# A decoder layer on one core: its beginning rearranged, the narrow gate load moved to chunk two, and two modulation sums spread over other units

## The chip, the core and the metric

The kernel runs on one NeuronCore of a Trainium2 chip. Its engines are TensorE (PE: matmuls, and PEld for the weight loads that run beside them), VectorE (DVE), ScalarE (ACT), GpSimd (POOL) and SyncE (SP, which here only issues loads and stores). The metric is the time of one execution on the device in microseconds.

## What is computed

One layer of a hybrid decoder, for one sequence of 256 tokens with 2048 channels, in float32. Cut to what matters:

```python
mod = silu(c) @ w_mod + b_mod                  # (2048) x (2048, 6*2048)
sh_m, sc_m, g_m, sh_f, sc_f, g_f = split(mod, 6)
h = rmsnorm(x, mix_pre_w) * (1 + sc_m) + sh_m
proj = h @ w_in                                # 48 tiles of 128 columns, and 16 more columns: a_lr
y_conv = cb * causal_dwconv3(cc * cx, conv_w)
log_a = log_sigmoid(a_lr @ gate_w2 + gate_b) / 16
y_gla = gla_chunked(q, k, v, log_a)            # then a norm for each head, times silu(r)
x = x + g_m * rmsnorm(concat(y_conv, y_gla) @ w_out, mix_post_w)
h = rmsnorm(x, ffn_pre_w) * (1 + sc_f) + sh_f
g, val = split(causal_dwconv3(h @ w_up, ffn_conv_w), 2)
x = x + g_f * rmsnorm((silu(g) * val) @ w_down, ffn_post_w)
```

All weights are read once from HBM. The modulation vector is needed in six parts: sh_m and sc_m (called the first modulation below) before the first projection, g_m (the second, "g") before the first residual, sh_f and sc_f (the third, "f" and "f2" for its two halves), g_f at the end.

## The kernel before, in words

**Products in three parts.** PE works in a fast format that keeps fewer bits (fp32r). To keep float32 precision each weight is split into a high part (`high`, a cast on ACT, L140) and a low part (`low`, the difference, on DVE, L145), and so are the activations (`act_high`, `act_low`, L380). A product is then high x high, high x low and low x high: L490, L491 and L492 in the input projection, L753 to L755 in the output and down products, L897 and L899 (two halves packed in one) in the up product. A few places use full float32 matmuls, among them L282 (columns of the modulation), L361 (transposes of x) and L436 (the product with the gate's 16 narrow columns, `alr_w`).

**Modulation.** The row of the modulation is summed on DVE: for each of 16 slices j of `w_mod`, one instruction adds c_act[j] times the slice to an accumulator (`mod_steps`, `stt` at L136). Each partition holds a share of the sum; a product with ones (L282) adds the shares and turns the row into columns (`mod_columns`: `products`, then `columns`, L285). For the first modulation this happens in four pieces, one for each chunk of the contraction; the pieces for chunks two to four, and g, f, f2, are spread over units (`spread`), with the list MODS giving the unit numbers at which one ends and the next begins.

**Chunks and units.** The input projection contracts over 2048 channels in four chunks (`CHUNKS`: 2, 4, 5 and 5 tiles of 128 channels). Chunk one runs over all 48 output tiles before chunk two begins. A unit is a group of two to four output tiles in a chunk, with its own weight load. Chunk one has units 0 to 11, chunk two 12 to 23, chunk three 24 to 41, chunk four 42 to 59; units 60 to 75 are the output product, then come the up and down products. A unit of chunk one has 24 matmuls, one of chunk two 48, one of the output product mostly 24 of double width.

**Order.** Every engine runs its instructions in program order, and `drive` writes that order. For unit i it issues: the unit's `early` list (mostly modulation steps), the load and the cast of weight i+2 (`prep`), the low part of weight i+1 (`low`), a `pre` list, the matmuls, a `mid` list, what earlier units have due (`fin`, the evacuation of PSUM), a `late` list. So DVE has the low part of a unit to do while PE works on the unit before, and a modulation step stands ahead of it in the same queue. All large loads are issued by SP in this same order; a load waits until its buffer is free. Loaded weights and modulation slices share six buffers ("raw"); high and low parts have three each ("wh", "wl"); most other tiles are slots of a pool of twenty ("big").

**The beginning.** `steps0` loads and sums the first piece (16 slices, in loads of four and then two slices). x is loaded in two halves of 128 tokens, at steps 0 and 8 (`XLD`), squared and scaled (`norm_squares`, `rstd_of`, L1013 to L1015) after steps 3 and 14 (`NLD`), and its first two tiles are transposed into PSUM. Then come the narrow load of `alr_w` (L1016, 128 partitions x 16 pieces of 64 bytes), the columns, and `modulate_chunk(0)`: ACT scales the transposed tiles (L367), casts them (L376), DVE takes the low part (L380), PE makes the gate's product for this chunk (L436). `drive` begins with the load and split of weight 0 and the load of weight 1.

**Between chunks.** In the unit before the last of a chunk the next chunk's columns are made and the next tiles of x transposed and modulated (`cols`, `mod0`, `LEAD` = 2); behind the last unit stand the low parts of the activations and the gate's products (`second`), and in the middle of the next chunk's first unit their sum (`third`, L446).

Of the kernel before, what the change touches and what calls it, by code (L numbers as in the profile page):

```python
# [36 lines left out]
XLD = (0, 8)  # L37
NLD = (3, 14)
# [3 lines left out]
MODS = (10, 21, 31, 46, 70)  # L42
# [7 lines left out]
NHF = 3  # L50

# [52 lines left out]
def layer_kernel(ctx: ExitStack, tc, x, c, w_mod, b_mod, mix_pre_w, mix_post_w, w_in, conv_w, gate_w2, gate_b,  # L104
# [47 lines left out]
    nc.scalar.activation(c_act, c_sb, AF.Silu)  # L152

# [3 lines left out]
    def mod_steps(s0, n, a, w, nj, first=False):  # L157
# [3 lines left out]
        def step(j):  # L161
            if j == 0:
# [3 lines left out]
                if first:  # L166
                    cur["b"] = slot([1, n, w])
                    nc.gpsimd.dma_start(cur["b"], b_mod_v[:, s0:s0 + n, a:a + w])
                else:
                    nc.gpsimd.memset(acc, 0.0)  # L170
                    nc.gpsimd.dma_start(acc[0:1, :, :], b_mod_v[:, s0:s0 + n, a:a + w])
# [8 lines left out]
            src, cj = cur["r"][:, j % m, :, :], c_act[:, j:j + 1]  # L180
            if first and j == 0:
                nc.vector.tensor_scalar_mul(cur["acc"], src, cj)
            else:
                stt(cur["acc"], src, cj, cur["acc"])
            if first and j == 3:
                nc.vector.tensor_add(cur["acc"][0:1], cur["acc"][0:1], cur["b"])
# [3 lines left out]
    accs0, steps0 = mod_steps(0, 2, 0, CHUNKS[0] * P, 4 if CHUNKS[0] < 3 else 2, True)  # L190

    ident = col(P, "ident")
    nc.scalar.dma_start(ident, ident_in)
# [3 lines left out]
    nc.scalar.copy(ones_r, ones)  # L197
    eps_t = col(1, "eps_t")
    nc.gpsimd.memset(eps_t, EPS)
# [218 lines left out]
    def modulate_chunk(ci, ash, early=None):  # L418
# [3 lines left out]

        def first():
            for kts in pairs(k0, k1):
                ps = early.pop(0) if early else turn_norm(xs, kts)
                hf = hf0[:, kts[0]:kts[-1] + 1, :] if ci == 0 else hf_tile()
# [5 lines left out]
        def second():  # L432
            ps = bank([P, T])
            for kts, hf, parts in kept:
                for i, k in enumerate(kts):
                    nc.tensor.matmul(ps[:16, :], alr_w[:, k, :], hf[:, i, :], start=(k == k0), stop=(k == k1 - 1))  # L436
                if parts:
                    act_low(*parts)
            kept.append(ps)

        def third():
            ps = kept.pop()
            if ci == 0:
                nc.vector.tensor_copy(alr[:16, :], ps[:16, :])
            else:
                nc.vector.tensor_add(alr[:16, :], alr[:16, :], ps[:16, :])  # L446

        return first, second, third

    def in_units(ci):  # L450
# [10 lines left out]
        def unit(tiles, plain):  # L461
# [3 lines left out]
            def prep():  # L465
                r = raw_tile([P, n, m * P])
# [9 lines left out]
            def mm():  # L476
                w = cur["w"]
                for o, nt in enumerate(tiles):
                    if nt // 2 not in banks:
                        banks[nt // 2] = bank([P, 2, T])  # L480
                    ps = banks[nt // 2][:, nt % 2, :]
# [19 lines left out]
        return [unit(g, i in (PLAIN, FULL1, FULL2, FULL)[ci]) for i, g in enumerate(groups)]  # L501
# [501 lines left out]
    for j, f in enumerate(steps0):  # L1003
        f()
        if j in XLD:
            load_x(XLD.index(j))
        if j == 0:
            load_small()
        if j in NLD:
            t = NLD.index(j)  # L1010
            r = rstd_of(norm_squares(t, f"n1{t}"), 4, f"n1{t}")
            e = CHUNKS[0] * P
            nc.vector.tensor_scalar_mul(xs[t][0][:, :e], xs[t][0][:, :e], r)  # L1013
            nc.scalar.activation(xs[t][0][:, e:], xs[t][0][:, e:], AF.Copy, scale=r)
            nc.scalar.activation(xs[t][1], xs[t][1], AF.Copy, scale=r)  # L1015
    nc.sync.dma_start(alr_w, w_in[:, 6144:6160].rearrange("(k p) n -> p k n", p=P))  # L1016
    small_columns()
# [3 lines left out]
    ash, products, columns = mod_columns(accs0, CHUNKS[0], pre_c[:, :CHUNKS[0]], "ash0")  # L1021
    products()
    columns()
    for f in modulate_chunk(0, ash, early):
        f()

    chunks = [in_units(ci) for ci in range(len(CHUNKS))]
# [8 lines left out]
    for ci in range(1, len(CHUNKS)):  # L1036
# [10 lines left out]
        def mod0(ci=ci, st=st):  # L1047
# [79 lines left out]
    def second_norm():  # L1127
# [28 lines left out]
        for g, m in ((4, 4), (8, 3), (12, 3)):  # L1156
            products(range(g, g + 4))
            keep_busy(banks[3], m)
# [33 lines left out]
    def keep_busy(ps, n):  # L1192
# [157 lines left out]
```

## Time and profile before

| | us |
|---|---|
| median of 3 runs | 1216.56 (1216.52 to 1217.66) |
| the profiled execution | 1216.94 |
| its span | 1215.1 |
| PE busy | 1178.0 (97%) |
| DVE busy | 946.2 (78%) |
| ACT busy | 570.4 (47%) |
| POOL busy | 34.7 (3%) |

The profile shows one execution. Times in its rows count from the start of the span. In a row of the order of instructions the first number is the start, the second the time from the start of the first to the end of the last of the instructions merged, then come engine, line, operation, tiles, count, and in brackets the idle time before and what ended it. In a table of stretches stand the busy time and count for PE, PEld, DVE, ACT and POOL, then the granted clock of PE (1.00 is full), the busy share of the DMA engines, and GB/s. In a list of waits stand the total, the number of times and the longest. In a list of loads stand the count, the size of one, and the time from issue to landing.

### The profile page before, as it was taken

The page shows a single profiled execution, that of the slowest core. Times are in us where ns is not written, and L with a number is a line of the kernel's source. Part 1 is how long each engine was busy: PE and PEld are TensorE (multiplying, and loading weights), DVE is VectorE, ACT ScalarE, POOL GpSimd, SP SyncE. Part 2 cuts the span into 40 slices and gives each one's busy share as a digit, 9 for nine tenths or more (in the row PEclk, how much of TensorE's full clock was granted, in tenths as well). Part 3 has the DMA queues.
Part 4 walks back from the last instruction along what each step waited for, and adds up shares of the span by engine and source line. Part 5 has one row for each costly group of instructions (what it writes and reads, how often), then busy time and mean ns, then how long its engine had stood idle before and what let it go on. Part 6 is the DMA issues. An engine that isn't in the chain of part 4 may idle for free.

```text
span 1215.1 us, 17130 instructions
## 1 busy us (share of the span) xinstructions
PE 1178.0 (97%) x7003; PEld 1040.8 (86%) x7003; DVE 946.2 (78%) x968; ACT 570.4 (47%) x662; POOL 34.7 (3%) x52
## 2 busy tenths in 40 slices
PE   2999999999999999999999999999999999999997
PEld 1999999999997888888888888888888888888885
DVE  5899999999999886984598979698876665444463
ACT  5563422443474446444554545544544543433452
POOL 2000020000001001000000000000000000000000
PEclk9999999999999999999999999999999999999999
DMA  9999899996699886996667767767664665555522
GB/s 305 386 385 388 310 360 391 398 346 213 201 339 368 321 339 222 361 347 218 237 208 242 257 227 235 251 221 267 223 229 155 239 252 182 207 180 201 194 84 70
DMA packets 128046, 320.73 MB, mean 264 GB/s; under 512 B 8341, under 2 KB 35685, under 8 KB 118240
## 3 DMA queue, kind: packets, MB, share of 16 engines
q1 hardware_dynamic: 125360, 312.63, 72.5%
q0 software_dynamic: 2320, 6.94, 1.6%
q8 instruction: 55, 0.90, 0.3%
q14 instruction: 23, 0.19, 0.0%
q10 hardware_dynamic: 288, 0.07, 0.0%
HBM read 315.42 MB, written 4.19 MB: 263 GB/s over the span
## 4 chain that ended last, share of the span: by engine, by line
PE 91%; DVE 4%; DMA 3%; issue 1%; ACT 1%; SPq 0%; DVEq 0%; ACTq 0%
PE ps L897 27%; PE ps L899 14%; PE ps L753 9%; PE ps L754 9%; PE ps L755 9%; PE ps L490 6%; PE ps L492 6%; PE ps L491 6%; DMA raw<-in_w_mod_dram 2%; PE ps L585 1%; PE ps L487 1%; DVE wl L145 1%; PE ps L282 1%; DVE big L136 1%; DVE macc L136 1%
## 5 line engine op out<-in xcount | busy, mean ns | idle before, releaser
L140 ACT CAST wh<-raw 128x2048 fp32r<-128x2048 f32 (+3 forms) x202 | 366.1, 1815 | 507.7 <-PE ps L897 195.3
L145 DVE TENSOR_TENSOR wl<-raw,wh 128x2048 fp32r<-128x2048 f32 (+3 forms) x202 | 437.1, 2166 | 141.8 <-ACT wh L140 141.8
L897 PE MATMUL ps<-big,wh 128*128 128x512 f32 x1400 | 494.8, 398 | 0.0
L899 PE MATMUL ps<-big,wl 128*128 128x256 f32 x1400 | 393.2, 281 | 1.1 <-DVE wl L145 1.1
L897 PEld LDWEIGHTS ps<-big,wh 128*128 128x128 f32 x1400 | 263.0, 188 | 64.7
L899 PEld LDWEIGHTS ps<-big,wl 128*128 128x128 f32 x1400 | 264.5, 189 | 1.5 <-DVE wl L145 1.5
L492 PE MATMUL ps<-big,wl 128*128 128x256 f32 x733 | 209.8, 286 | 2.7 <-DVE wl L145 2.7
L490 PE MATMUL ps<-big,wh 128*128 128x256 f32 x733 | 211.4, 288 | 0.2 <-ACT wh L140 0.2
L491 PE MATMUL ps<-big,wh 128*128 128x256 f32 x733 | 209.4, 286 | 0.0
L136 DVE SCALAR_TENSOR_TENSOR macc<-raw,c_act,macc 128x2048 f32<-128x2048 f32 (+1 forms) x96 | 199.2, 2075 | 3.0 <-DMA raw<-in_w_mod_dram 2.8
L753 PE MATMUL ps<-wh,big 128*128 128x512 f32 x456 | 178.4, 391 | 0.0
L754 PE MATMUL ps<-wl,big 128*128 128x512 f32 x456 | 177.5, 389 | 0.0
L755 PE MATMUL ps<-wh,big 128*128 128x512 f32 x456 | 177.5, 389 | 0.0
L492 PEld LDWEIGHTS ps<-big,wl 128*128 128x128 f32 x733 | 142.6, 195 | 3.6 <-DVE wl L145 3.6
L490 PEld LDWEIGHTS ps<-big,wh 128*128 128x128 f32 x733 | 142.7, 195 | 2.7 <-ACT wh L140 1.4
L491 PEld LDWEIGHTS ps<-big,wh 128*128 128x128 f32 x733 | 142.8, 195 | 0.1
L755 PEld LDWEIGHTS ps<-wh,big 128*128 128x128 f32 x456 | 85.6, 188 | 17.9
L754 PEld LDWEIGHTS ps<-wl,big 128*128 128x128 f32 x456 | 85.6, 188 | 17.9 <-issue 0.2
L753 PEld LDWEIGHTS ps<-wh,big 128*128 128x128 f32 x456 | 85.6, 188 | 17.9 <-issue 0.2
L136 DVE SCALAR_TENSOR_TENSOR big<-big,fcw,big 128x254 f32<-128x254 f32 (+1 forms) x176 | 72.1, 474 | 0.0
L823 DVE TENSOR_TENSOR big<-big,ps 128x256 f32<-128x256 f32 x88 | 31.1, 415 | 48.4 <-ACT big L821 48.4
L416 DVE TENSOR_TENSOR big<-big,ps 128x512 f32<-128x512 f32 x66 | 43.1, 676 | 0.6 <-PE ps L492 0.5
(199 smaller groups left out, 668.9 us busy)
## 6 DMA issues: line engine op xcount, KB each, us to landing
raw<-in_w_up_dram SPq DMA_DIRECT2D x88, 1024.0 KB, 5.4
raw<-in_w_mod_dram SPq DMA_DIRECT2D x64, 1024.0 KB, 6.8
raw<-in_w_down_dram SPq DMA_DIRECT2D x44, 1024.0 KB, 4.8
raw<-in_w_in_dram SPq DMA_DIRECT2D x24, 960.0 KB, 8.1
raw<-in_w_mod_dram SPq DMA_DIRECT2D x32, 640.0 KB, 7.3
raw<-in_w_out_dram SPq DMA_DIRECT2D x16, 1024.0 KB, 6.9
raw<-in_w_in_dram SPq DMA_DIRECT2D x12, 1024.0 KB, 8.2
raw<-in_w_mod_dram SPq DMA_DIRECT2D x22, 512.0 KB, 6.9
```

The source lines that it names most:

```text
L136: nc.vector.scalar_tensor_tensor(o, a, s, b, op0=op0, op1=op1)
L140: nc.scalar.copy(hi, raw)
L145: nc.vector.tensor_sub(lo, raw, hi.bitcast(F32))
L416: nc.vector.tensor_add(dst, dst, ps)
L490: nc.tensor.matmul(ps, w[0][:, kk, cs], ht[:, k % 2, 0, :], start=st, stop=False)
L491: nc.tensor.matmul(ps, w[0][:, kk, cs], ht[:, k % 2, 1, :], start=False, stop=False)
L492: nc.tensor.matmul(ps, w[1][:, kk, cs], ht[:, k % 2, 0, :], start=False, stop=sp)
L753: nc.tensor.matmul(ps, a[:, i, 0, ts_], w[0][:, kk, ns], start=st, stop=False)
L754: nc.tensor.matmul(ps, a[:, i, 0, ts_], w[1][:, kk, ns], start=False, stop=False)
L755: nc.tensor.matmul(ps, a[:, i, 1, ts_], w[0][:, kk, ns], start=False, stop=sp)
L897: nc.tensor.matmul(pss[o], wh[:, kk, cs], h2[k // 2][:, k % 2, :, :], start=(first and kk == 0), stop=False)
L899: nc.tensor.matmul(pss[o][:, 1, :], wl[:, kk, cs], h2[k // 2][:, k % 2, 0, :], start=False, stop=(last and kk == 3))
```

## The change

- **Beginning.** The rows of the first piece are loaded and summed in loops of their own (`first_load`, `first_step`). x's halves are loaded behind the second and the third load of rows, squared in two pieces of 1024 each instead of four of 512, and scaled one step after the root is asked for (`NLD` = 9, 13). The last four slices of rows and the weights of units 0 to 3 go to slots of the large pool instead of the raw buffers. The table for the square root is loaded at the start by one small activation. The load of the identity moves from ACT's queue to POOL's, and the small vectors are loaded later. The scaling of the rest of x (`rest_of_rows`) moves behind units 1 and 3.
- **Matmuls on ones.** 9, 1 and 3 matmuls of 512 columns (`keep_busy`, `BUSY`) stand behind the first transposes, the second transposes and the products for the columns.
- **Chunk one's activations.** ACT writes the high part at once from PSUM, DVE the full value, then the low part (`at_once`). Weight 0 is loaded and split before the columns. Unit 0 runs its three parts one after the other over all tiles (`by_parts`).
- **Gate.** The narrow load moves to the `early` list of chunk two's first unit. The gate's products of chunks one and two are made together in the middle of chunk two's unit 4 (`GATE1`; six products, unit 16 in all), and their sum in the middle of the next. Those of chunks three and four stay behind the last unit of the chunk before.
- **Spread.** MODS goes from (10, 21, 31, 46, 70) to (10, 21, 31, 54, 74): the steps of g run over units 31 to 53 instead of 31 to 45, those of f over 54 to 73 instead of 46 to 69. f2 stays at 70 to 74 and on into the up product.

```diff
-XLD = (0, 8)
-NLD = (3, 14)
+XLD = (4, 8)
+NLD = (9, 13)
-MODS = (10, 21, 31, 46, 70)
+MODS = (10, 21, 31, 54, 74)
+BUSY = (9, 1, 3)
+WSLOT = 4
+GATE1 = 4
...
-    units[0].prep()
-    units[0].low()
-    units[1].prep()
...
+    eps_t = col(1, "eps_t")
+    nc.vector.memset(eps_t, EPS)
+    warm = col(1, "warm")
+    nc.scalar.activation(warm, eps_t, AF.Sqrt)
...
+    def first_load(j, m, tile):
+        r = tile([P, m, 2, W0])
+        for s in range(2):
+            nc.sync.dma_start(r[:, :, s, :], w_mod_v[:, j:j + m, s, 0:W0])
+        for i in range(m):
+            first_rows[j + i] = r[:, i, :, :]
...
-    nc.scalar.dma_start(ident, ident_in)
+    nc.gpsimd.dma_start(ident, ident_in)
+    nc.gpsimd.dma_start(first_b, b_mod_v[:, 0:2, 0:W0])
...
+    def keep_busy(n):
+        ps = bank([P, 4, P])
+        for i in range(n):
+            nc.tensor.matmul(ps, ones_r, busy_r, start=i == 0, stop=i == n - 1)
...
+        def at_once():
+            n = CHUNKS[0]
+            for kts in pairs(k0, k1):
+                ps, hf = early.pop(0), hf0[:, kts[0]:kts[-1] + 1, :]
+                d = hts[kts[0] // 2] = slot([P, 2, 2, T], F32R)
+                ab = [(ash[:, n + k:n + k + 1], ash[:, k:k + 1]) for k in kts]
+                for i, (a, b) in enumerate(ab):
+                    nc.scalar.activation(d[:, i, 0, :], ps[:, i, :], AF.Identity, bias=b, scale=a)
+                for i, (a, b) in enumerate(ab):
+                    nc.vector.tensor_scalar(hf[:, i, :], ps[:, i, :], a, b, op0=ALU.mult, op1=ALU.add)
+                    h32.setdefault(ci, {})[kts[i]] = hf[:, i, :]
+                act_low(d, hf)
+                kept.append((kts, hf, None))
...
+    def gate_products():
+        ps = bank([P, T])
+        for i, (k, h) in enumerate(gate_terms):
+            nc.tensor.matmul(ps[:16, :], alr_w[:, k, :], h, start=i == 0, stop=i == len(gate_terms) - 1)
...
-                r = raw_tile([P, n, m * P])
+                r = slot([P, n, m * P]) if ci == 0 and tiles[0] < 24 + 4 * WSLOT and tiles[0] >= 24 else raw_tile([P, n, m * P])
...
+    for j in range(0, 12, 4):
+        first_load(j, 4, raw_tile)
         if j in XLD:
             load_x(XLD.index(j))
+    for j in range(12, KT, 2):
+        first_load(j, 2, slot)
+    load_small()
...
+    ss = halves_squared(0)
+    for j in range(KT):
+        first_step(j)
+        if j == 7:
+            small_columns()
         if j in NLD:
             t = NLD.index(j)
+            rs[t] = std_of(ss, 2, f"n1{t}")
+            if t == 0:
+                ss = halves_squared(1)
+        if j - 1 in NLD:
+            norm_rows(NLD.index(j - 1))
     early = [turn_norm(xs, kts, None, (0,)) for kts in pairs(0, CHUNKS[0])]
+    keep_busy(BUSY[0])
     for kts, ps in zip(pairs(0, CHUNKS[0]), early):
         turn_norm(xs, kts, ps, (1,))
+    keep_busy(BUSY[1])
...
     products()
+    keep_busy(BUSY[2])
+    chunks[0][0].prep()
+    chunks[0][0].low()
     columns()
+    first, second = modulate_chunk(0, ash, early)
+    first()
+    second()
+    chunks[0][1].prep()
+    chunks[1][0].early.append(lambda: nc.sync.dma_start(alr_w, w_in[:, 6144:6160].rearrange("(k p) n -> p k n", p=P)))
+    chunks[0][1].late.append(lambda: rest_of_rows(0))
+    chunks[0][3].late.append(lambda: rest_of_rows(1))
...
-        seconds.append((us[-LEAD + 1].late,
-                        lambda st=st: st["m"][1]()))
-        seconds.append((chunks[ci][0].mid, lambda st=st: st["m"][2]()))
+        seconds.append((us[-LEAD + 1].late, lambda st=st: st["m"][1]()))
+        seconds.append((us[-LEAD + 1].late if ci > 1 else chunks[1][GATE1].mid, gate_products))
+        seconds.append((chunks[ci][0 if ci > 1 else GATE1 + 1].mid, gate_sum))
```

More of the change, by code (lines that the diff above doesn't have):

```diff
@@ L432, in second, with gate_sum @@
         def second():
[L433 removed]
             for kts, hf, parts in kept:
[L435 to L436 removed]
                 if parts:
                     act_low(*parts)
[L439 to L448, printed above, removed]
+                for i, k in enumerate(kts):
+                    gate_terms.append((k, hf[:, i, :]))
+        return first, second
+    gate_terms, gate_ps = [], []
+    def gate_products():
+        ps = bank([P, T])
+        for i, (k, h) in enumerate(gate_terms):
+            nc.tensor.matmul(ps[:16, :], alr_w[:, k, :], h, start=i == 0, stop=i == len(gate_terms) - 1)
+        gate_ps.append((ps, gate_terms[0][0] == 0))
+        gate_terms.clear()
+    def gate_sum():
+        ps, is_first = gate_ps.pop(0)
+        if is_first:
+            nc.vector.tensor_copy(alr[:16, :], ps[:16, :])
+        else:
+            nc.vector.tensor_add(alr[:16, :], alr[:16, :], ps[:16, :])
     def in_units(ci):
```

93 lines of the change are left out of this document (54 added, 39 removed).

## The prediction

> **What bounds the kernel now.** I read the page first, then the list of what TensorE waited for, then the stretches of time, then the order of instructions around the places the change touches. Units are numbered through: 0 to 11 is chunk one, 12 to 23 chunk two, 24 to 41 three, 42 to 59 four, 60 to 75 the output product.
>
> ```profile
> span 1215.1 us, 17130 instructions
> PE 91%; DVE 4%; DMA 3%; issue 1%; ACT 1%; SPq 0%; DVEq 0%; ACTq 0%
> ```
> ```profile
> PE ps L492 <- DVE wl L145: 2.7, 3, 1.3
> ```
> ```profile
> 80.00:90.00 10.00, 10.00 (x86) 10.00 (x85) 9.90 (x9) 4.35 (x5) 0.00 (x0) 1.00 1.05 390
> ```
>
> TensorE (PE) carries 91% of the chain that ended last. After its first weight product it waits for VectorE (DVE) three times, 2.7 us in all. From 80 us on it runs 86 matmuls in 10 us, and DVE and the DMA engines are full beside it, at 390 GB/s. So after 80 us a microsecond is gained only by taking work off PE, and lost wherever DVE falls behind by more than its lead. Before that, PE first waits for the beginning:
>
> ```profile
> 23.61 0.75 DVE L136 SCALAR_TENSOR_TENSOR big<-raw,c_act,big 128x512 f32<-128x512 f32 x1
> ...
> 27.32 1.89 PE L436 MATMUL ps<-big,alr_w 128*16 128x256 f32 x4 [0.98 <-ACT big L367]
> ...
> 29.38 0.58 PE L490 MATMUL ps<-big,wh 128*128 128x256 f32 x1 [0.16 <-ACT wh L140]
> ```
>
> The modulation rows are summed at 24.36, the gate's products (L436) end at 29.2, the first weight product starts at 29.38. Chunk one then hangs on the stream of loads. In it each unit brings a 0.5 MB weight and 1.6 modulation rows of 0.5 MB, 1.3 MB; at 390 GB/s that is 3.4 us, and its 24 matmuls at 0.12 us are 2.9 us. The rows where DVE stands idle for a load show it:
>
> ```profile
> 62.17 2.60 DVE L136 SCALAR_TENSOR_TENSOR big<-raw,c_act,big 128x1024 f32<-128x1024 f32 x2 [0.31 <-DMA raw<-in_w_mod_dram]
> ...
> 70.12 1.55 DVE L136 SCALAR_TENSOR_TENSOR macc<-raw,c_act,macc 128x1280 f32<-128x1280 f32 x1 [1.56 <-DMA raw<-in_w_mod_dram]
> ...
> 75.47 1.28 DVE L380 TENSOR_TENSOR big<-hf,big 128x512 fp32r<-128x512 f32 x2
> ```
>
> The second of these stands ahead of chunk two's modulation columns (L285), and those lead through ScalarE (ACT) to the low parts of chunk two's activations (75.47, the first ready at 76.1), without which unit 12 can't go past its first matmul.
>
> **The change part by part.** *The beginning.* Rows first: x is loaded after the second group of rows, the table load for the square root is done at the start, the first chunk's four gate records (1.89 us) leave, weight 0 is split ahead of the columns. The narrow load (alr_w, 128 KB in pieces of 64 bytes) leaves the SP queue between the last rows and weight 0:
>
> ```profile
> alr_w<-in_w_in_dram SPq DMA_DIRECT2D x1, 128.0 KB, 7.8
> ```
> ```profile
> 20.00:22.00 2.00, 0.00 (x0) 0.00 (x0) 1.70 (x4) 0.38 (x2) 0.00 (x0) 1.00 0.96 147
> 22.00:24.00 2.00, 0.24 (x1) 0.25 (x2) 1.60 (x5) 0.95 (x2) 0.00 (x0) 1.00 0.75 169
> ```
> ```profile
> 16.10 5.84 SPq L467 DMA_DIRECT2D raw<-in_w_in_dram  x2
> ```
>
> Where it goes through, the engines move 147 and 169 GB/s: 632 KB in 4 us where 390 GB/s would be 1560, a loss of 2.4 us, and 0.3 us more for its own bytes. SP, which issues weights 0 and 1 in that time, is held 5.84 us for two loads, so part of the hole is a queue with nothing else in it. All later loads come 2.7 us sooner.
>
> ```profile
> raw<-in_w_in_dram SPq DMA_DIRECT2D x1, 512.0 KB, 9.2
> ```
> ```profile
> 24.19 1.13 ACT L1015 ACTIVATE big<-big,n 128x1024 f32<-128x1024 f32 x1
> ...
> 26.71 1.02 ACT L367 ACTIVATE big<-ps,ash 128x256 f32<-128x256 f32 x2 [1.39 <-DVE ash L136]
> ...
> 28.29 1.99 ACT L140 CAST wh<-raw 128x1024 fp32r<-128x1024 f32 x2
> ...
> 29.66 1.20 DVE L145 TENSOR_TENSOR wl<-raw,wh 128x1024 fp32r<-128x1024 f32 x1
> ```
>
> Weight 0 landed at 16.10 + 9.2 = 25.3, so now at 22.6; a cast of 1.0, a low part of 1.2, columns and one modulate of 0.5 each with their hand-overs put the first product at about 25.8, 3.6 sooner (29.38 before). The added instructions (13 matmuls on ones, three small ones on DVE) lie in time where PE and DVE wait for loads; the identity and the small vectors change from ACT's queue to POOL's or come later on POOL's, which has nothing else due; the direct high parts save ACT a cast; the scaling of the rest of x on ACT (two per half, 1.13 the longest) moves behind units 1 and 3, where ACT waits for loads between casts. Without that cover each would cost its 1.1.
>
> But chunk one ends when its loads end. Its last modulation row and everything up to the load behind 70.12 shift by 2.7, so the low parts are ready at 73.4 instead of 76.1, and unit 12 starts there. Before:
>
> ```profile
> 75.10 1.90 PE L436 MATMUL ps<-hf,alr_w 128*16 128x256 f32 x8
> ```
> ```profile
> 76.93 0.39 PE L490 MATMUL ps<-big,wh 128*128 128x256 f32 x1
> ```
>
> The 1.9 us of gate products in front of unit 12 were nearly free: they covered the wait for the low parts. Their removal there gains only 76.93 - 76.1 = 0.8. Unit 12 starts 3.5 us sooner.
>
> Then two bills come. First the narrow load: it now stands on SP ahead of the rows and weight that unit 12 issues, so its hole falls at about 72 to 75 us and puts the loads behind it back by 2.0 (the queue is not empty behind it now) to 2.7. DVE lives from hand to mouth there:
>
> ```profile
> 80.52 1.55 DVE L136 SCALAR_TENSOR_TENSOR macc<-raw,c_act,macc 128x1280 f32<-128x1280 f32 x1
> ...
> 83.78 2.27 DVE L145 TENSOR_TENSOR wl<-raw,wh 128x2048 fp32r<-128x2048 f32 x1
> ```
> ```profile
> 71.70 2.05 SPq L176 DMA_DIRECT2D raw<-in_w_mod_dram  x2
> ```
> ```profile
> raw<-in_w_mod_dram SPq DMA_DIRECT2D x2, 640.0 KB, 8.7
> ```
>
> The row used at 80.52 was issued at 71.70 and landed 8.7 later, at 80.4. With the hole in front, DVE is back on its old times, and the low part of unit 14 still ends near 85.9, where PE now wants it at 85.2. That leaves unit 14 about 2.8 sooner than before (88.45 = 76.93 + 2 x 5.76), up to 3.5 with the short hole. Second, six gate products stand behind unit 16, where PE is full: 12 records at 1.90 / 8 = 0.23 are 2.75 us. The unit length is from two casts that start when PE frees a weight:
>
> ```profile
> 94.39 1.91 ACT L140 CAST wh<-raw 128x2048 fp32r<-128x2048 f32 x1 [3.21 <-PE ps L491]
> 100.15 1.91 ACT L140 CAST wh<-raw 128x2048 fp32r<-128x2048 f32 x1 [3.85 <-PE ps L491]
> ```
>
> 3.5 - 0.7 - 2.75 = 0.05 with the long hole, 0.7 with the short one. I take **-0.6**, bounds 0 and -1.3 (loads 0.6 us faster besides).
>
> A word on the clock. Before, PE ran unit 0 and part of unit 1 at 0.213 us for a matmul, until 36.85, and half rate came back once after 65 us:
>
> ```profile
> 36.63 0.41 PE L491 MATMUL ps<-big,wh 128*128 128x256 f32 x1
> 36.85 0.34 PE L492 MATMUL ps<-big,wl 128*128 128x256 f32 x1
> ```
> ```profile
> 65.00:70.00 5.00, 4.97 (x34) 5.00 (x35) 3.56 (x3) 2.69 (x4) 0.00 (x0) 0.77 1.01 381
> ```
>
> The matmuls on ones are to lift it sooner; 28 matmuls, from the end of the first wait (30.9) to 36.85, at 0.213 - 0.12 would be 2.6 us. [...] By the rows above they are not, since the stream of loads sets chunk one's end: 2.6 us there only make PE wait longer at units 4 to 10.
>
> *The spread.* By the lists of places, the second modulation's (g) 16 rows go from units 31-45 to 31-52, the third's (f) from 46-68 to 54-72. Each is a DVE instruction of 2.34 us and a 1 MB load. In 31-45 five fewer run. PE lost next to nothing there:
>
> ```profile
> 220.00:225.00 5.00, 4.95 (x41) 4.74 (x41) 5.00 (x4) 1.80 (x1) 0.00 (x0) 1.00 1.03 399
> ```
>
> Three matmuls of 44, **-0.3** (0 to -0.3). What is late next is at unit 60, whose low part ends within 0.2 us of its use:
>
> ```profile
> 348.83 0.20 DVE L700 RECIPROCAL grs<-grs 128x8 f32<-128x8 f32 x1 [1.25 <-ACT grs L699]
> 349.50 2.34 DVE L136 SCALAR_TENSOR_TENSOR macc<-raw,c_act,macc 128x2048 f32<-128x2048 f32 x1
> ...
> 356.85 2.28 DVE L145 TENSOR_TENSOR wl<-raw,wh 128x2048 fp32r<-128x2048 f32 x1
> ```
> ```profile
> 359.29 0.40 PE ps L754
> ```
>
> Up to this low part the counts from unit 51 are old 5, new 7, of which one is made up before; so one more row, 2.34, of which the idle 1.25 hides part: 0.8 late at most, nothing if DVE comes with a lead. **+0.4** (0 to 1.0).
>
> In 70 to 72 three more rows stand beside those of f2, and 68's moves to 69, past the idle:
>
> ```profile
> 408.28 2.29 DVE L145 TENSOR_TENSOR wl<-raw,wh 128x2048 fp32r<-128x2048 f32 x1 [5.12 <-ACT wh L140]
> ...
> 424.08 2.28 DVE L145 TENSOR_TENSOR wl<-raw,wh 128x2048 fp32r<-128x2048 f32 x1
> ```
> ```profile
> 424.34 1.92 ACT L140 CAST wh<-raw 128x2048 fp32r<-128x2048 f32 x1 [3.33 <-PE ps L755]
> 429.78 1.92 ACT L140 CAST wh<-raw 128x2048 fp32r<-128x2048 f32 x1 [3.52 <-PE ps L755]
> ```
>
> A unit is 5.44 on PE; DVE now has 2.28 + 2 x 2.34 = 7.0 in each. Walking the order: low 70 ends at 417.9 (PE at 418.8), low 71 at 424.65 (424.3), low 73 at 435.9 (435.6), low 75 at 444.9 (444.8): 0.9 us of waits. What is left of DVE's lateness meets the second norm's residual:
>
> ```profile
> 454.07 1.42 DVE L136 SCALAR_TENSOR_TENSOR big<-big,ry,big 128x512 f32<-128x512 f32 x2
> ```
>
> It would come at 455.5. Together **+1.4**, bounds 0 (DVE arrives with a lead) and 4.6 (three times 7.0 - 5.44 with nothing absorbed). The loads themselves keep up: from 416 to 438 about ten of 1 MB at 2.7 us land just ahead of use.
>
> **Sum.** -0.6 - 0.3 + 0.4 + 1.4 = +0.9, against the profiled execution's 1216.94 (its span 1215.1 and 1.8 around it): 1217.8. That execution lies 0.4 above the median 1216.56, so I predict **1217.4**.
>
> **Rivals.** *The beginning passes through.* PE, not the loads, sets chunk one: 3.6 from the start, 2.6 from the clock, 0.75 of the first wait, less 2.75 - 1.90 more gate products on PE: 6.1 sooner at unit 17, and with +1.5 for the spread -4.6, 1211.9 after the same 0.4. For it: PE's later waits in chunk one were short (2.7 in all). Against: DVE's idle times for loads above. It decides if the loads gain well over 2.7 us, or the hole doesn't reappear. Chance 0.31. *The crowd at 70 to 72 is paid in full*: 4.6 instead of 1.4, and 1.0 at unit 60: 1221.2. It decides once DVE is more than the 2.3 us of one row late at unit 71, that is, if a load is late too. For it: 7.0 against 5.44. Against: 5.12 us of idle before, filled by 66 and 67. Chance 0.14. *The narrow load's hole falls on PE*: it starves the rows of chunk two by its whole 2.7 while nothing was gained in chunk one: 1217.4 + 2.7 = 1220.1. Chance 0.07. *It doesn't do what it says* for the clock: PE idles between the nine matmuls on ones and the last transposes, and unit 0 runs at half rate again; this costs nothing, since loads set the end, and belongs to the forecast.
>
> **How the numbers follow.** A measurement here tells about 0.2% (2.4 us) from no change: faster is below 1214.1, slower above 1219.0. The forecast has 0.48, its own range 1215.4 to 1219.0. The first rival and a little of the forecast's lower end make faster 0.32; the second and third, less a little of the third, make slower 0.20; same is 0.48. The range takes in half of the first rival and most of the second, 1211.8 to 1220.8.
>
> **What would show it.** First product at 25 to 26.5 us; no hole in GB/s at 20 to 24 and one at 70 to 76; unit 12 at about 73.4; the 12 gate records behind unit 16, and unit 17 within 1 us of its old time (105.7); DVE with idle time at 195 to 225; short PE waits for L145 near 359, 424 and 435; the second norm's residual about 1 us late. I am wrong if unit 17 starts 3 us or more early, or if PE waits over 3 us in 415 to 460.

## The result, and the profile after

The changed kernel takes 1225.32 us (median of 6 runs, 1222.41 to 1226.68) against 1217.18 for the kernel before beside it: ratio 1.0062, 95% interval 1.0049 to 1.0075. Measured again later it was 1.0052 (1.0039 to 1.0065). It is slower, by some 6 to 8 us; the forecast was 1217.4. The profiled execution took 1224.8.

The head of the page and the engines' shares of the chain that ended last, in the changed kernel:

```profile
span 1223.0 us, 17140 instructions
...
PE 83%; DVE 8%; DMA 4%; issue 2%; ACT 2%; SPq 0%; DVEq 0%; ACTq 0%
```

PE held 91% of the chain before and holds 83% now, DVE 8% instead of 4%. The list of what PE waited for (total, times, longest), below the two waits of the beginning, names the places:

```profile
...
PE ps L548 <- DVE wl L145: 3.6, 4, 1.9
PE ps L810 <- DVE wl L145: 3.4, 2, 3.1
PE ps L547 <- DVE big L401: 1.8, 1, 1.8
PE ps L1290 <- DVE big L1242: 1.2, 1, 1.2
```

Lines have moved: L546 to L548 are the old L490 to L492, L809 to L811 the old L753 to L755, L401 the old L380, L303 the column products (L282), L773 the old L717. The second row is new: a wait of 3.1 us for one low part, that of unit 60. New too is a granted clock (third number from the end) under 1 in these three stretches. The kernel before, and then the changed kernel:

```profile
130.00:140.00 10.00, 10.00 (x87) 10.00 (x87) 10.00 (x11) 2.65 (x2) 0.00 (x0) 1.00 0.98 348
230.00:240.00 10.00, 10.00 (x87) 10.00 (x88) 10.00 (x9) 4.09 (x6) 0.00 (x0) 1.00 1.04 397
360.00:370.00 10.00, 10.00 (x48) 8.26 (x47) 10.00 (x9) 6.25 (x5) 0.00 (x0) 1.00 0.91 324
```

```profile
130.00:140.00 10.00, 10.00 (x79) 10.00 (x78) 10.00 (x11) 2.23 (x2) 0.00 (x0) 0.89 0.99 351
230.00:240.00 10.00, 10.00 (x75) 10.00 (x74) 6.00 (x7) 1.90 (x2) 0.00 (x0) 0.83 1.02 381
360.00:370.00 10.00, 6.90 (x26) 5.38 (x25) 10.00 (x8) 4.47 (x5) 0.00 (x0) 0.83 0.79 286
```

"Busy" doesn't show this loss: in 230 to 240 PE is busy for all 10 us in both, but with 75 matmuls instead of 87. Where the 7.9 us of span come in is read by following one instruction through both orders:

| PE instruction | before | changed | difference |
|---|---|---|---|
| first weight product | 29.38 | 25.73 | -3.6 |
| transposes for chunk two | 71.26 | 66.42 | -4.8 |
| first product of unit 17 | 105.7 | 105.31 | -0.4 |
| column products for chunk three | 134.63 | 134.20 | -0.4 |
| transposes for chunk three | 142.62 | 143.68 | +1.1 |
| column products for chunk four | 229.60 | 230.37 | +0.8 |
| transposes for chunk four | 237.23 | 239.48 | +2.2 |
| transposes ahead of unit 60 | 358.45 | 359.68 | +1.2 |
| transposes ahead of unit 61 | 364.52 | 370.33 | +5.8 |
| product behind 418 us | 418.38 | 424.21 | +5.8 |
| f's columns, first | 443.18 | 449.85 | +6.7 |
| last transposes of the second norm | 466.77 | 474.59 | +7.8 |

Steps of +1.5 behind each of two column products, +4.6 at unit 60, and 0.8 and 1.2 at the end. 1.0 comes back in two steps of 0.5, near 296 and 312 us. That is a gain of the spread: between 238 and 335 us the kernel before and e1 (below: the old spread) each wait for ACT twice, 0.5 us of listed idle time in all, and the changed kernel and e2 (the new spread alone) not at all; e2 makes the same two steps against the kernel before.

### The profile page after: what moved, and what is told of

Same layout as the page of the kernel before. It is cut to its first block, busy times and chain, and to the rows that moved or that the text cites. A ratio compares the mean times of both kernels' runs of the same rounds, so it can differ in the third digit from the quotient of the medians.

```text
span 1223.0 us, 17140 instructions
## 1 busy us (share of the span) xinstructions
PE 1184.1 (97%) x7016; PEld 1045.5 (85%) x7016; DVE 947.5 (77%) x972; ACT 568.0 (46%) x653; POOL 35.2 (3%) x52
## 4 chain that ended last, share of the span: by engine, by line
PE 83%; DVE 8%; DMA 4%; issue 2%; ACT 2%; SPq 0%; DVEq 0%; ACTq 0%
PE ps L953 27%; PE ps L955 13%; PE ps L810 8%; PE ps L811 8%; PE ps L809 8%; PE ps L546 5%; PE ps L547 5%; PE ps L548 5%; DMA raw<-in_w_mod_dram 4%; DVE wl L145 2%; DVE macc L136 2%; DVE big L136 1%; DMA big<-in_w_in_dram 1%; PE ps L303 1%; PE ps L485 1%
## 5 line engine op out<-in xcount | busy, mean ns | idle before, releaser
L140 ACT CAST wh<-raw 128x2048 fp32r<-128x2048 f32 (+3 forms) x198 | 362.0, 1831 | 503.6 <-PE ps L953 195.6
L145 DVE TENSOR_TENSOR wl<-raw,wh 128x2048 fp32r<-128x2048 f32 (+3 forms) x198 | 432.4, 2186 | 138.8 <-ACT wh L140 138.8
L548 PE MATMUL ps<-big,wl 128*128 128x256 f32 x725 | 208.3, 287 | 3.7 <-DVE wl L145 3.6
L546 PE MATMUL ps<-big,wh 128*128 128x256 f32 x725 | 209.8, 289 | 0.0
L809 PE MATMUL ps<-wh,big 128*128 128x512 f32 x456 | 178.9, 392 | 0.0
L811 PE MATMUL ps<-wh,big 128*128 128x512 f32 x456 | 178.0, 390 | 0.0
L548 PEld LDWEIGHTS ps<-big,wl 128*128 128x128 f32 x725 | 141.8, 196 | 4.7 <-DVE wl L145 4.7
L546 PEld LDWEIGHTS ps<-big,wh 128*128 128x128 f32 x725 | 141.9, 196 | 1.7 <-PE ps L485 0.8
L811 PEld LDWEIGHTS ps<-wh,big 128*128 128x128 f32 x456 | 86.0, 189 | 18.0
L809 PEld LDWEIGHTS ps<-wh,big 128*128 128x128 f32 x456 | 85.9, 188 | 17.8 <-issue 0.2
```

Source lines behind the costliest of these rows:

```text
L140: nc.scalar.copy(hi, raw)
L145: nc.vector.tensor_sub(lo, raw, hi.bitcast(F32))
L546: nc.tensor.matmul(ps, w[0][:, kk, cs], ht[:, k % 2, 0, :], start=st, stop=False)
L548: nc.tensor.matmul(ps, w[1][:, kk, cs], ht[:, k % 2, 0, :], start=False, stop=sp)
L809: nc.tensor.matmul(ps, a[:, i, 0, ts_], w[0][:, kk, ns], start=st, stop=False)
L811: nc.tensor.matmul(ps, a[:, i, 1, ts_], w[0][:, kk, ns], start=False, stop=sp)
```

## The experiments

**Theory A:** the loss comes from the spread, by DVE's rows in front of the low part of unit 60. **Theory B:** it comes from the beginning and the clock behind it. Four kernels with other lists of places tell them apart.

```diff
 e1 (changed kernel)  -MODS = (10, 21, 31, 54, 74)  +MODS = (10, 21, 31, 46, 70)
 e2 (kernel before)   -MODS = (10, 21, 31, 46, 70)  +MODS = (10, 21, 31, 54, 74)
 e3 (changed kernel)  -MODS = (10, 21, 31, 54, 74)  +MODS = (10, 21, 31, 46, 74)
 e4 (changed kernel)  -MODS = (10, 21, 31, 54, 74)  +MODS = (10, 21, 31, 54, 70)
```

> The changed kernel with the spread as it was before (10, 21, 31, 46, 70): the beginning, the gate and the matmuls on ones alone. Theory A, the loss comes from the spread: TensorE's wait of 3.1 us for unit 60's low part, the half clock behind it and the waits behind 415 us go, and 1217 to 1218.5 us is left (the beginning's own -0.4, and up to 1.5 us for each window at half clock behind the column products of chunks three and four). Theory B, the beginning and the clock behind it are the cause: 1221 us or more, with unit 60 starting over 3 us late without any wait at unit 60.

> The kernel before with the new spread (10, 21, 31, 54, 74) alone. Theory A: a wait of about 3 us for unit 60's low part (L754 for L145), a window at half clock behind it (1.5 us), about 0.8 us of waits in 415 to 450 and 1.2 us at the second norm, less 1.0 us of ScalarE waits that go in 290 to 330: 1217.2 + 5.6, about 1222.5 us. Theory B: within 1.5 us of the kernel before, 1216 to 1218.7.

> The changed kernel with (10, 21, 31, 46, 74): g packed as before, f over 46 to 73, so the rows in 70 to 73 are as in the changed kernel and those in 54 to 59 are not. If the cost is at unit 60 (rows in front of the gate norm's reciprocal and of the low part): that wait is under 1 us, and the time is 1219 to 1220.5. If it is the crowd behind unit 70: 1222 or more, with DVE's lateness at the second norm unchanged.

> The changed kernel with (10, 21, 31, 54, 70): g spread as in the changed kernel, f in each of the units 54 to 69, none of it in 70 to 73. If the cost is at unit 60: the wait for its low part stays or grows (3 us or more; six rows of f instead of five stand ahead of it), the residual of the second norm is on its old time relative to unit 60, and the time is 1222 to 1225. If it is the crowd behind unit 70: 1219 or less.

| | median us | ratio to before (95%) |
|---|---|---|
| e1 beginning alone | 1217.76 | 1.0006 (0.9995 to 1.0017) |
| e2 spread alone | 1222.83 | 1.0052 (1.0037 to 1.0066) |
| e3 f from 46 to 73 | 1218.62 | 1.0012 (1.0002 to 1.0022) |
| e4 f from 54 to 69 | 1225.31 | 1.0074 (1.0059 to 1.0090) |

Theory A holds for the greater part: the spread alone makes the kernel before about as slow, and with f begun at 46 again the loss is nearly gone, though two of the changed kernel's three rows in units 70 to 73 stay. (By the lists e3 has 70 and 72, the changed kernel 70, 71 and 72, so the test isn't quite as clean as expected. e3 came out 0.4 us below its range, e4 0.3 us above.) e2 and e4 show waits of 3.1 and 3.9 us at unit 60; e1 and e3 none there.

**What makes unit 60 late.** In the changed kernel DVE's order ahead of that low part, and ACT's, are these:

```profile
348.60 2.34 DVE L136 SCALAR_TENSOR_TENSOR macc<-raw,c_act,macc 128x2048 f32<-128x2048 f32 x1
350.86 0.68 DVE L437 TENSOR_TENSOR big<-big,ps 128x512 f32<-128x512 f32 x1
351.46 0.19 DVE L756 RECIPROCAL grs<-grs 128x8 f32<-128x8 f32 x1
...
358.40 0.69 DVE L583 TENSOR_TENSOR big<-big,big 128x512 fp32r<-128x512 f32 x1 [1.90 <-ACT big L579]
359.01 2.35 DVE L136 SCALAR_TENSOR_TENSOR macc<-raw,c_act,macc 128x2048 f32<-128x2048 f32 x1
361.27 2.29 DVE L145 TENSOR_TENSOR wl<-raw,wh 128x2048 fp32r<-128x2048 f32 x1
```

```profile
353.06 3.01 ACT L765 ACTIVATE big<-ps,grs 128x256 f32<-128x256 f32 x8
355.91 1.95 ACT L140 CAST wh<-raw 128x2048 fp32r<-128x2048 f32 x1
357.71 0.67 ACT L579 CAST big<-big 128x512 fp32r<-128x512 f32 x1
```

A row of f (348.60) stands ahead of the gate norm's reciprocal, so ACT's scaling (L765) and its cast (L579) come later, DVE idles 1.90 us for that cast, and then another row (359.01) stands ahead of the low part. One experiment moves the first row, one the second.

```diff
 e5
+    fmoved = allin[57].mid.pop()
...
+    allin[57].late.append(fmoved)
 e6
+    allin[59].mid.insert(0, allin[59].early.pop())
```

> The changed kernel with one row of f moved: from the middle of unit 57, in front of the gate norm's reciprocal (L756), to behind it and behind the first step of the convolution. Theory A1, the wait at unit 60 is mostly a chain through ScalarE (reciprocal late by a row, then L765, the cast L579, and VectorE idle for it 1.9 us): the reciprocal comes about 2.3 us sooner, the idle goes, the wait of L810 for unit 60's low part falls from 3.1 to 0.9 to 1.6 us, the window at half clock behind it mostly goes, and the time is 1221 to 1223.3. Theory A2, it is only the count of rows in front of the low part: the wait stays at 2.6 or more, and the time at 1224 to 1226.

> The changed kernel with the other row moved: from in front of the low part of unit 60 to behind it. A1 and A2 both: the wait at unit 60 falls to about 0.8 us. A2 (VectorE's whole work counts): the row then delays the low part of unit 61, where a wait of 2 to 2.5 us appears, with the half clock, and the time stays at 1223.5 to 1225.5. If only the place counts: no wait over 1 us at unit 61, 1220.5 to 1222.5.

e5 took 1225.11 us (1.0066, 1.0054 to 1.0079), e6 1221.97 (1.0049, 1.0035 to 1.0063). In e5 DVE and PE:

```profile
347.83 0.20 DVE L756 RECIPROCAL grs<-grs 128x8 f32<-128x8 f32 x1 [1.25 <-ACT grs L755]
...
355.25 0.69 DVE L583 TENSOR_TENSOR big<-big,big 128x512 fp32r<-128x512 f32 x1
355.85 2.34 DVE L136 SCALAR_TENSOR_TENSOR macc<-raw,c_act,macc 128x2048 f32<-128x2048 f32 x1
358.12 2.28 DVE L145 TENSOR_TENSOR wl<-raw,wh 128x2048 fp32r<-128x2048 f32 x1
```

```profile
360.46 0.69 PE L810 MATMUL ps<-wl,big 128*128 128x512 f32 x1 [2.65 <-DVE wl L145]
```

The idle for the cast is gone, the idle of 1.25 ahead of the reciprocal is back, and the wait falls only from 3.10 to 2.65: the chain through ACT (A1) is worth 0.45 us, the count of rows (A2) the rest. In e6 the wait is cut in two, at units 60 and 61:

```profile
359.97 0.50 PE L810 MATMUL ps<-wl,big 128*128 128x512 f32 x1 [0.85 <-DVE wl L145]
```

```profile
367.90 0.50 PE L810 MATMUL ps<-wl,big 128*128 128x512 f32 x1 [1.74 <-DVE wl L145]
```

Together 2.6 us again, as A2 has it. But no half clock follows, and the time is lower than A2 expected (1223.5 to 1225.5). That pointed to the clock.

**The clock.** Behind the column products of chunk three, in the changed kernel:

```profile
134.20 2.29 PE L303 MATMUL ps<-ones,macc 128*128 128x2 f32 x20
...
137.63 0.28 PE L547 MATMUL ps<-big,wh 128*128 128x256 f32 x1
137.75 0.34 PE L548 MATMUL ps<-big,wl 128*128 128x256 f32 x1
137.89 0.41 PE L546 MATMUL ps<-big,wh 128*128 128x256 f32 x1
138.10 0.42 PE L547 MATMUL ps<-big,wh 128*128 128x256 f32 x1
```

20 matmuls of two columns, 2.29 us; 1.4 us after their end the starts of the products are 0.21 us apart instead of 0.12. The trace keeps the granted clock as a list of stretches: each fall before the end of the execution lasts 3.41 us (twice, in e5 and e16, two such lengths in a row), and all starts lie a whole multiple of 3.41 us apart (here 45.67, 72.98, 137.83, 233.40, 363.11). So the falls of a profile lie on one grid of windows of 3.41 us, and it lies differently from execution to execution: the first start, less whole windows, goes from 0.28 to 3.37 us over the 18 profiles (1.30 in the changed kernel's, 2.82 in that of the kernel before). e7 makes the products in two halves, a unit apart.

```diff
 e7 (e1, and)
-        us[-LEAD].early.append(cols)
+        if ci == 1:
+            us[-LEAD].early.append(cols)
+        else:
+            us[-LEAD - 2].mid.append(cols_a)   # products(range(n))
+            us[-LEAD - 1].mid.append(cols_b)   # products(range(n, 2 * n))
 e8 (e1, and)
-    nc.sync.dma_start(alr_w, w_in[:, 6144:6160].rearrange("(k p) n -> p k n", p=P))
+    nc.sync.dma_start(alr_w, w_in[0:P, 0:256].rearrange("p (k n) -> p k n", n=16))
```

> The beginning alone (e1) with the two-column products (L303) of chunks three and four made in two halves, behind units 20 and 21 (38 and 39) instead of all in front of unit 22 (40). If they, a stretch of 2 us of very small matmuls, bring the windows at half clock near 137 and 233 us: no such window in 100 to 400, the mean clock over the runs rises from 0.9958 to 0.997, and the median falls by 0.7 to 1.5 us, to 1216 to 1217. If these windows have another cause: within 0.5 us of e1 (1217.8), with clock 0.996.

> The beginning alone (e1) with the narrow load's 128 KB taken in rows of 1 KB from the first 256 columns of w_in's first 128 rows instead of 2048 pieces of 64 bytes: other values go into the gate, the work stays the same. The prediction's hole (2.0 to 2.7 us behind 70 us) is then gone: unit 17 up to 2 us sooner and the time 1215.8 to 1217 if loads still set the start of chunk two; within 0.5 us of e1 (1217.8) if VectorE or TensorE does.

e7 took 1215.89 us (1215.13 to 1216.99; ratio 0.9992, 0.9984 to 1.0001). In its profile no fall in 100 to 400 is left, the median is 1.9 under e1's and the spread 1.9 us instead of e1's 4.9. The mean clock rose less than expected, from 0.9958 to 0.9964. A fall lowers it by 0.0014 (half of 3.41 us in 1216), so that is 0.4 of a fall in each execution, about 0.7 us; the rest of the 1.9 is within the noise of the two ratios, or has another cause. Its stretches:

```profile
130.00:140.00 10.00, 10.00 (x87) 10.00 (x86) 10.00 (x11) 1.79 (x1) 0.00 (x0) 1.00 1.00 352
230.00:240.00 10.00, 10.00 (x85) 9.87 (x85) 10.00 (x10) 6.04 (x10) 0.24 (x1) 1.00 1.03 393
```

e8 tests the narrow load's hole. In the changed kernel, and then in e8, with the GB/s at the end of each row:

```profile
68.00:70.00 2.00, 2.00 (x19) 2.00 (x18) 2.00 (x2) 1.97 (x4) 0.00 (x0) 1.00 1.10 227
70.00:72.00 2.00, 0.43 (x4) 0.23 (x2) 2.00 (x2) 1.97 (x4) 0.00 (x0) 1.00 0.65 126
```

```profile
68.00:70.00 2.00, 2.00 (x20) 2.00 (x18) 2.00 (x5) 1.53 (x3) 0.00 (x0) 1.00 1.05 387
70.00:72.00 2.00, 1.00 (x9) 0.79 (x7) 2.00 (x2) 1.97 (x5) 0.00 (x0) 1.00 1.04 391
```

The hole is there and e8 fills it, yet its time is 1217.29 (1.0009, 0.9999 to 1.0019), that of e1, and in its profile unit 17 begins at 105.78, with a fall of the clock behind 73 as in the changed kernel (105.31): loads don't set chunk two.

Four more: the clock held through the wait at unit 60 (e9), the beginning without its matmuls on ones (e10), and the split columns in the kernel before (e11) and in the changed kernel (e12).

```diff
 e9 (changed kernel, and; e14 the same with 24)
+    def hold_here():
+        ps = bank([P, P])
+        for _ in range(40):
+            nc.tensor.matmul(ps, ones_r, ones_r, start=True, stop=True)
+    allin[60].pre.append(hold_here)
 e10 (e7, and)
-BUSY = (9, 1, 3)
+BUSY = (0, 0, 0)
```

> The changed kernel with 40 matmuls of 128 columns on ones in front of unit 60's products: they fill most of TensorE's wait for unit 60's low part (3.1 us) and change nothing in what it waits for. If the half clock behind that wait is a cost of its own (about 1.6 us): no window at half clock in 355 to 380, unit 60 takes 9 us instead of 10.65 between its first transposes and the next unit's, and the median is 1222.8 to 1224.3 instead of 1225.3. If the clock falls for another reason, or the lost time is VectorE's alone: window and time stay, 1225 to 1226.

> e7 without the 13 matmuls on ones of the beginning (0, 0, 0 instead of 9, 1, 3). By the prediction they are worth nothing, since the loads set the end of chunk one: unit 0 then runs at half rate, unit 12 and unit 17 start within 0.6 us of e7's, and the median is within 0.6 us of 1215.9. If they are worth the 2.6 us of the half rate: 1217.5 or more.

> The kernel before with the column products of chunks three and four in two halves, as in e7. If they cause windows at half clock there too, in some executions: median 1215.5 to 1216.7 against 1217.0, with a smaller spread than the 5 us of the kernel before. If this kernel seldom has them: no difference within 0.5 us. Compared with e7 it gives the worth of the beginning alone, free of these windows: e7 lower by 0 to 1.

> The changed kernel, spread and all, with the column products of chunks three and four in two halves. The windows near 137 and 233 us are the beginning's part of the loss: they go, and the median is 1222.3 to 1224.2 instead of 1225.3; the wait and the half clock at unit 60 stay. If the time stays at 1225 or more, these windows weren't part of the loss.

e9: 1224.84 (1.0048), not conclusive, as the 40 matmuls took 4.66 us, longer than the wait. e10: 1216.43 (0.9991, 0.9981 to 1.0000), e7's ratio: no worth of the matmuls on ones shows in the time. (In its profile unit 17 is 2.8 us later than in e7, against 0.6 expected; 0.6 of that is lost at the first products, and in 50 to 60 the loads run at 341 and 334 GB/s instead of 390 and 384. That these are the reason for the rest isn't shown.) e11: 1217.03 (0.9990, 0.9980 to 1.0001), a small gain at most, with a spread of 4.4 us that stays, unlike e7's. It was also to give the worth of the beginning alone: e7's 0.9992 against this 0.9990 is +0.2 us, about 1.6 to either side, where e7 lower by 0 to 1 had been expected. e12: 1221.69 (1.0030, 1.0018 to 1.0042), 3.6 under the changed kernel (2.7 to 3.9 by the ratios to the kernel before), more than expected. Its unit 60 is a control that came by itself: the same wait, and no half clock behind it.

```profile
360.40 0.50 PE L810 MATMUL ps<-wl,big 128*128 128x512 f32 x1 [3.10 <-DVE wl L145]
360.74 0.40 PE L811 MATMUL ps<-wh,big 128*128 128x512 f32 x1
360.98 0.40 PE L809 MATMUL ps<-wh,big 128*128 128x512 f32 x1
```

In the changed kernel:

```profile
359.68 0.60 PE L773 MATMUL ps<-ident,big 128*128 128x128 f32 x4
...
363.62 0.79 PE L810 MATMUL ps<-wl,big 128*128 128x512 f32 x1 [3.10 <-DVE wl L145]
364.21 0.63 PE L811 MATMUL ps<-wh,big 128*128 128x512 f32 x1
364.63 0.63 PE L809 MATMUL ps<-wh,big 128*128 128x512 f32 x1
```

A unit of this size without a wait takes 5.93 us from its transposes to the next ones (unit 61 of the changed kernel). Unit 60, with the same wait of 3.10, takes 9.33 in e12, but 10.65 here: 1.3 us for the clock alone.

Then two questions that were left: the crowd behind unit 70, and the price of the clock.

```diff
 e13 (e12, and)
-    spread(fsteps, [u for i, u in enumerate(allin) if MODS[3] <= i < MODS[4]])
+    spread(fsteps, [u for i, u in enumerate(allin) if 60 <= i < MODS[4]])
```

> e12 (the changed kernel with split column products) with f's 16 rows over units 60 to 73 only: none stands in front of unit 60's low part, and more than before stand in 60 to 73. If the spread's cost is the rows in 54 to 59: no wait at unit 60, and 1216 to 1217.5, near e7 (1215.9) and over 4 us under e12 (1221.7). If the crowd behind unit 70 has a price of its own: waits for low parts between 380 and 450 us and a late second norm, 1219 to 1222.

> e9 with 24 matmuls on ones instead of 40, 2.7 us at 0.112 us each, inside the wait of 3.1 us. Unit 60 then takes 9.0 to 9.4 us from its transposes to the next ones (10.65 in the changed kernel, 9.33 in e12, whose wait wasn't followed by half clock), no window in 355 to 380, and the median is 1223.4 to 1224.4. If it is at 1225 or more, the half clock there isn't a cost of its own.

e13: 1223.09 (1.0050, 1.0035 to 1.0064). That is above both of its ranges. Nothing waits at unit 60, but the crowd has a price of its own:

```profile
422.24 7.00 DVE L136 SCALAR_TENSOR_TENSOR macc<-raw,c_act,macc 128x2048 f32<-128x2048 f32 x3
429.15 2.28 DVE L145 TENSOR_TENSOR wl<-raw,wh 128x2048 fp32r<-128x2048 f32 x1
```

```profile
431.49 0.50 PE L810 MATMUL ps<-wl,big 128*128 128x512 f32 x1 [3.35 <-DVE wl L145]
```

Rows of f from unit 60 on, by the lists: 6 before, 8 in e3, 11 in the changed kernel, 16 in e13. Losses between unit 61's transposes and those of the second norm, against the kernel before: 0.3 us in e3, 2.0 in the changed kernel (0.8 and 1.2), 7.8 in e13, with waits of 1.3, 3.35 and 0.97 us and a fall of the clock behind the second. e14 has the clock held as meant:

```profile
357.03 2.88 PE L1163 MATMUL ps<-ones_r 128*128 128x128 f32 x24
359.74 0.45 PE L809 MATMUL ps<-wh,big 128*128 128x512 f32 x1
360.62 0.50 PE L810 MATMUL ps<-wl,big 128*128 128x512 f32 x1 [0.43 <-DVE wl L145]
```

Unit 60 takes 9.31 us, as expected. The median, 1220.97 (1.0033, 1.0022 to 1.0044), is lower than that explains. In e14's profile the column products happen to bring no fall either, so series were not alike; the last series has both remedies and the changed kernel side by side. e15 is e12 with e14's `hold_here`.

> The changed kernel with the column products split (e12) and 24 matmuls on ones in unit 60's wait (e14). What is left of the loss is then the waits: 3.1 us at unit 60 and about 2 us behind unit 70, less 1 us in 290 to 330: ratio to the kernel before 1.0025 to 1.0037, about 1220 to 1221.5. If the two remedies add up as measured one by one (-3.6 and -4.3): 1217.5 or less.

> The changed kernel as it is, in one series with the run of both remedies. If its windows at half clock differ from series to series: 1222 to 1224.5, with a mean clock over 0.993. If they belong to it: 1224.5 to 1226, clock 0.991 to 0.993, as in its first six runs.

e15: 1219.45 (1.0022, 1.0011 to 1.0032), clock 0.997. e16: 1223.92 (1.0052), clock 0.992, and in its profile the changed kernel's falls again. Its clock is the one expected if the falls belong to the changed kernel; its median lies in the range of the other expectation, so that question is only half answered. The remedies don't simply add up. Side by side, in one series, the clock costs 1.0052 less 1.0022, 3.7 us, with about 2 to either side; the first series of the changed kernel (1.0062) would make it 4.9. Both of its profiles have falls near 73, 137, 233 and 363 us, and one is worth about 1.5 us (16 matmuls at 0.21 instead of 0.12), so not quite all of them reach the end. The waits of the spread cost 1.0022 less 0.9992 (e7), 3.7 us; the trace has 3.1 + 0.8 + 1.2 - 1.0 = 4.1. No version was found that is surely faster than the kernel before: the intervals of e7, e10 and e11 end at 1.0001, 1.0000 and 1.0001.

## Why the prediction was wrong

- **The beginning** was read rightly in most of its marks, and in one by luck. The first product came at 25.73 (forecast 25.8), and the list of holes is as forecast: none at 20 to 24, one at 68 to 72 (forecast 70 to 76).

```profile
20.00:22.00 2.00, 2.00 (x6) 1.55 (x6) 1.96 (x4) 0.29 (x1) 0.00 (x0) 1.00 1.06 383
22.00:24.00 2.00, 1.70 (x11) 0.97 (x10) 1.59 (x5) 1.05 (x1) 0.00 (x0) 1.00 1.04 385
```

Unit 12 passed its first matmul at 72.28 (73.4), the 12 gate records stand behind unit 16, and unit 17 began at 105.31 (within 1 us of 105.7). One reason in it was wrong: the hole in chunk two was billed at 2.0 to 2.7 us and costs nothing (e8). What ate the gain of 4.6 at unit 12 were the gate products, 2.75, and a window at half clock behind 72.98, 1.5. So it was luck that unit 17 stood so near its old time: a fall of the clock took the place of the bill for the hole. In e1, whose profile has no such fall, unit 17 came at 104.14, 1.6 us early. The worth of the beginning, forecast at -0.6, can't be told from nothing: e1 as it is gives +0.7 (between -0.6 and +2.1), and e7 against e11, both with split columns, +0.2.
- **The rival that the beginning passes through** (unit 17 6.1 us sooner) was not it: 0.4 here, 1.6 in e1. Neither sign of being wrong that the prediction names came either, as unit 17 isn't 3 us early and PE's only listed wait in 415 to 460 is 0.3. The loss fell at unit 60 and behind the column products, which neither sign watches.
- **The matmuls on ones** lift the clock: unit 0's products at 29 us start 0.12 apart, where the kernel before has 0.21; without them its first eight products take 2.07 us (e10) instead of 1.21 (e7). In the time that is worth nothing that shows, as forecast (e10).
- **The spread of g** did what was read: DVE's busy time in 195 to 225 fell from 29.99 to 27.43 us. The credit of 0.3 was too small, as 1.0 more came back near 296 and 312.
- **Unit 60 is the step that failed in size**: "one more row, 2.34, of which the idle 1.25 hides part: 0.8 late at most", +0.4, with a bound of 1.0. It is 3.1. The idle was no slack: it was DVE's wait for the gate norm's root, and with a row ahead of it, it comes back some 5 us later as 1.90 for ACT's cast. To the row (2.34) and this difference (0.65) comes 0.4 that DVE had lost before: the row of f near 330 us starts at 329.05 in the kernel before and here at

```profile
330.69 2.35 DVE L136 SCALAR_TENSOR_TENSOR macc<-raw,c_act,macc 128x2048 f32<-128x2048 f32 x1
```

which is 1.6 later, while PE is 1.2 later. Less the lead of 0.2 this makes 3.2.
- **The clock is the term that was missing.** The step on the clock looked at the beginning alone and then priced every lateness as itself. The column products (2.29 us) and the wait at unit 60 (3.10 us), stretches of sparse PE work, had 3.41 us at a granted clock of 0.5 behind them. In the profile the two behind the column products cost 1.5 us each and the one at unit 60 1.3, 4.3 in all; by e15 and e16 it is 3.7, with about 2 to either side. That is about half of the miss of 7.9.
- **Units 70 to 75 and the second norm**: +1.4 was forecast, 2.0 came. 1.2 of it is at the norm as named. Two low parts come late where 424 and 435 were named (at 430.59 and 441.79 on the changed kernel's clock); by the starts of the same matmuls in both kernels they cost 0.40 and 0.31, against 0.9 forecast. The rival of the full crowd (4.6) was not it, but e13 shows the mechanism with more rows.

## What to carry to other kernels

Before a row or a product is moved on a tuned kernel, count what stands ahead of each low part in every unit, and treat an engine's idle time as slack only if what it waits for doesn't depend on what you move. Look behind every new wait of PE and every block of tiny matmuls for a fall of the clock: here one stood behind 12 of 24 blocks of 2.29 us and behind 12 of 20 waits of 0.8 us and more, at 1.3 us (unit 60) to 1.5 us (column products) each. Breaking the block in two (e7, e12: halves of 1.18 us) or filling the wait (e14: 0.43 us of it were left) took the fall away here. A sum spread over more units crowds the sum behind it: f's 16 rows had 23 units before and have 19 now.

## What the runs showed of the hardware

In the table the clock fell behind sparse stretches that fill at most 2.91 of the 3.41 us of a window. Each trace is cut here into the grid that its own stretches of clock give; beside the largest part of a sparse stretch that lies in one window stands whether the next window was at half rate (waits are those of 0.8 us and more at unit 12 and at the output product):

| sparse stretch of PE | largest part in one window, us | clock fell |
|---|---|---|
| column products of chunks three and four, 2.29 us, 24 in 12 profiles | 2.08 to 2.29 (12 of them) | in all 12 |
| the same | 1.18 to 1.92 (12 of them) | in none |
| in halves, 1.18 us, 24 in 6 profiles | up to 1.18 | in none |
| waits for a low part, 12 in 10 profiles | 1.74 to 2.91 | in all 12 |
| the same, 8 in 7 profiles | 0.85 to 1.75 | in none |

The wait of 3.10 us in e12 is among the last: an edge of the grid cuts it into 1.64 and 1.46. The one in the changed kernel has 2.59 in one window. For waits the two lists touch: the clock fell behind 1.74 in e8, and not behind 1.74 (e6) and 1.75 (e3). So in these profiles it fell behind every block of tiny matmuls with 2.08 us or more in one window and behind every wait with more than 1.75; no block had between 1.92 and 2.08. The two waits of 3.10 us are equally long; the grid lies differently. One window at half rate costs about 1.5 us, an estimate from the 16 matmuls at 0.21 us instead of 0.12 and the steps of +1.5 behind the column products. That this makes equal executions differ is the author's estimate, and it isn't all of their spread: those of the changed kernel differ by over 4 us and those of e7 by less than 2, yet e11 and e15, with split columns too, still differ by 4.4 and 4.0.

The kernel before has the same column products; in its two profiles (its own and e2) they lie across an edge of the grid (at most 1.31 and 1.91 us in one window), and no fall follows. Over its executions it seems to meet some: splitting them (e11) lifts the mean clock from 0.9966 to 0.9977, 0.7 of a fall in each execution, about 1.1 us, and its time falls by 1.2. One would be expected, as two blocks are hit in 12 of 24 cases. In the changed kernel the same split (e12) lifts the mean clock from 0.9922 or 0.9925 to 0.9948, 1.7 to 1.9 falls. Why it meets more of them stays open.
